# Operands moved by 64 bytes, later spills, batched conditioning and tiles seeded in PSUM in a two-layer diffusion block

## The chip, the cores and the metric

The kernel runs on one core of a Trainium2 chip. The metric is device time in microseconds (us); lower is better. The kernel before took 1252.23, 1252.26 and 1252.82 us in three runs, a median of 1252.26.

Engines are named as in the profile: PE is TensorE's matmul queue and PEld its weight loads, DVE is VectorE, ACT ScalarE, POOL GpSimd, SP SyncE, whose queue issues nearly all of this kernel's DMAs. L123 is line 123 of the kernel.

## The reference, cut to what matters

Two layers work on 512 latent and 256 context tokens of width 1024. Layer 0 mixes tokens by pooling, layer 1 by attention; each is followed by an MLP with 4096 hidden columns. Layer 1 is the last, so its MLP sees latent tokens only.

```python
def ada_mods(cond, w, b):                     # w: 1024 x 6144
    m = (jax.nn.silu(cond) @ w + b)[..., None, :]
    return jnp.split(m, N_MOD, axis=-1)       # sh1, sc1, gt1, sh2, sc2, gt2
...
x = x + gt1 * rms_norm(y_lat, g_mix_post[i])
m_lat = sq_relu_mlp(modulate(rms_norm(x, g_mlp_pre[i]), sh2, sc2), w_mlp_in[i], w_mlp_out[i])
x = x + gt2 * rms_norm(m_lat, g_mlp_post[i])
...
def sq_relu_mlp(h, w_in, w_out):
    return jnp.square(jax.nn.relu(h @ w_in)) @ w_out
```

The conditioning `m` is made for two vectors, `c` (latent) and `c_ctx` (context), and depends on no token. Everything is fp32.

## The kernel before

**Tiles and number format.** Tokens lie in six tiles of 128 (t = 0 to 3 latent, 4 and 5 context). An fp32 product is made of three fp32r matmuls: each operand is split into a rounded `hi` (a ScalarE cast, L120) and a remainder `lo` (a VectorE subtract, L123), and hi·hi, hi·lo and lo·hi are added up in PSUM. A group of 256 hidden columns has w_in and w_out of 1 MB each; there are 16 groups (g).

**Buffers.** `ra` holds the split activations, `rb` the hidden values `hid` and one slot `unit[0]`. A tile `units` holds `unit[1]` and `unit[2]`, two slots of 2 x 2048 columns for split weights. In SBUF `ra`, `rb` and the later tile `sums` begin 32 bytes past a multiple of 128; `units` lies behind a small tile `phase` of 24 floats and begins 96 bytes past one, as do the work tiles, in which the diagonals of `gate_diag` lie too. Raw weights land in `rawp`, three buffers of 1 MB shared by w_in, w_out and w_ada.

**Layer 0's MLP.** The first group and part of the second run as ordinary products (`Inner`, L526). From then on w_in products take seven half-size products in place of eight (`Seven`): `weights_sums(g+1)` builds the combined weights on VectorE (L610 to L620), `sums()` (L561) the combined activations once, and PE multiplies them at L636 with 384 tokens as the moving operand. `out_mm` multiplies the hidden values of a tile with w_out (L731): 12 matmuls with a moving operand of 128x512 into two PSUM banks. `out_ev` adds the banks to `acc` in SBUF on VectorE (L742; a copy, L740, at g = 0). The pool `psB` has four banks, two tiles' worth, which `ada_fin` also uses. w_out of every group is split into `unit[2]`, in one cast and one subtract of 2048 columns. In layer 1 w_out's slots alternate between `ra` (even g) and `units` (odd g).

**Conditioning.** The first 20 pieces of w_ada (256 columns each) run on PE at the start (`ada_mm`, L212; `ada_sel`). The other 28 run on VectorE during layer 0's MLP: `ada_sum` loads 1 MB and makes 7 multiply-adds for each vector (L251), 14 for a dual piece (both vectors), 7 for a lone one (`c` only), then transposes and a reduction (L256). `ada_fin` turns the partial sums into columns with four small fp32 matmuls (L219) and one add (L229). Each g from 0 takes one dual and one lone piece while they last, through `extra0` (ahead of w_in's product) and `mid0` (in its middle); a piece's `ada_fin` comes one step after its sum.

**Spill.** `xr`, the residual stream (six tiles of 512 KB), goes to DRAM during layer 0's MLP, whose `sums` takes its place. The six stores are issued by SP at L703, each at a hand-written time of the list `st`, after the tile's `norm_s`; SP's queue also carries every weight load (L106). L988 loads xr back.

**Order.** The program is written for a scheduler that interleaves the engines' streams by priorities and its own model. Hand-written times (`Steps.at`) fix the order in which steps are handed to it; `keep_in_program_order` pins single instructions. `gate_diag` (L288) turns a gate into two diagonal matrices for matmuls; the one for layer 1's last gate stands in the output stage of attention (L1145).

Of the kernel before, what the change touches and what calls it, by code (L numbers as in the profile page):

```python
# [17 lines left out]
P = 128  # L18
# [35 lines left out]
def backbone(ctx: ExitStack, tc, x, c, ctx_in, c_ctx, w_ada, b_ada, g_mix_pre, g_mix_post,  # L54
# [34 lines left out]
    rb = const.tile([P, 10240], F32R, name="rb")  # L89
    phase = ctx.enter_context(tc.tile_pool(name="phase", bufs=1)).tile([P, 24], F32, name="phase")  # L90
    rawe = ExitStack()
# [22 lines left out]
    def sm_tile(tag):  # L114
        return small.tile([P, 8], F32, tag=tag, name=tag, bufs=2 if tag == "gc" else 8)

    def split(raw, hi, lo, pin=False, pool_hi=False, pool_lo=False, q=None):
        if q is not None:
            raw, hi, lo = (z[:, 512 * q:512 * q + 512] for z in (raw, hi, lo))
        a = gp.tensor_copy(hi, raw) if pool_hi else sc.copy(hi, raw)  # L120
        if pin:
            tc.keep_in_program_order(a)
        b = (gp if pool_lo else ve).tensor_tensor(out=lo, in0=raw, in1=hi, op=ALU.subtract)  # L123
        if pin:
            tc.keep_in_program_order(b)
# [3 lines left out]
    class Ring:  # L129
        def __init__(self, slots):  # L130
            self.slots, self.n = slots, 0

        def load(self, src, width, pin=False, wait=None):
            raw = raw_load(src, width, rawp)
            s = self.slots[self.n % len(self.slots)]
            self.n += 1
            hi, lo = s[:, 0:2048], s[:, 2048:4096]
            if wait is None:
# [64 lines left out]

    rowsd = {}

# [20 lines left out]

    def ada_out(i, m, j, ps, nc_):
        at = m * KT + 2 * j
        ve.tensor_tensor(out=mods[i][:, at:at + 2, 0:nc_], in0=ps.rearrange("p (b c) -> p b c", c=nc_),  # L229
                         in1=cols[:, i * 48 + at: i * 48 + at + 2].unsqueeze(2).broadcast_to([P, 2, nc_]),  # L230
                         op=ALU.add)
        if m in (SC1, SC2):
            s = 0 if m == SC1 else 1
            g0 = 96 + s * 16 + i * KT + 2 * j
            ve.scalar_tensor_tensor(out=avec[i][s][:, 2 * j:2 * j + 2, 0:nc_], in0=mods[i][:, at:at + 2, 0:nc_],
                                    scalar=1.0,
                                    in1=cols[:, g0:g0 + 2].unsqueeze(2).broadcast_to([P, 2, nc_]),
                                    op0=ALU.add, op1=ALU.mult)

    def ada_sum(i, m, j, nc_):  # L240
        raw = raw_load(w_ada[i, :, m * D + j * 256: m * D + (j + 1) * 256]
# [11 lines left out]
        for c, r in enumerate(rows):  # L253
            ve.transpose(raw[:, c, :], r)
        s = small.tile([P, 2, 8], F32, tag="part", name="part", bufs=2)
        ve.tensor_reduce(out=s[:, 0:nc_, :], in_=raw[:, 0:nc_, :].rearrange("p c (g q) -> p c g q", q=32),  # L256
                         axis=AX.X, op=ALU.add)
        rowsd[i, m, j] = s, nc_
# [301 lines left out]

    def sums():  # L561
        held.close()
        S["held"] = ExitStack()
        f = S["held"].enter_context(tc.tile_pool(name="sums", bufs=1, side="right")).tile([P, 8712], F32R, name="sums")[:, 0:8704]
        u = unit[0]
# [131 lines left out]
    for n, t in enumerate(order):  # L697
# [4 lines left out]
        st.at([57.98, 62.18, 66.38, 70.58, 74.78, 78.98][n], norm_s, t, (False, False, False, False, False, False)[n])  # L702
        st.at([61.98, 66.18, 70.38, 74.58, 78.78, 82.98][n], lambda t: sy.dma_start(spill[:, t], xr[:, t]), t)  # L703
        st.at([60.08, 64.28, 68.48, 73.066, 77.266, 81.466][n], norm_c, t, (False, True, False, False, False, False)[n], (False, True, True, True, True, False)[n])
# [8 lines left out]
    def mlp(i, inner, rg, hids, order, extra, mid, last, before_last):  # L713
# [6 lines left out]
        def out_mm(parts, t, cols=HALVES):  # L720
            at_ = place_of[t] if i == 0 else t
            ts_ = slice(at_ * P, (at_ + 1) * P)
            pss = [psB.tile([P, 512], F32, tag="b", name="pso") for _ in cols]
            seq = [(a, f, w) for (_, (hi, lo), (wH, wL)) in parts for f in range(2)
                   for a, w in ((hi, wH), (hi, wL), (lo, wH))]
            order = [(n, h) for n in range(len(seq)) for h in range(len(cols))]
            if len(parts) > 1:
                order.sort(key=lambda z: (z[0] >= (9 if cols == HALVES else 0), z[1]))
            for n, h in order:
                a, f, w = seq[n]  # L730
                te.matmul(pss[h][:, 0:cols[h][1]], a[:, f, ts_], w[:, f, cols[h][0]:sum(cols[h])],  # L731
                          start=(n == 0), stop=(n == len(seq) - 1))
            pso[t] = pss

        def out_ev(parts, t, cols=HALVES):
            pss = pso[t]
            for (c0, w), ps in zip(cols, pss):
                d = accv[:, t, c0:c0 + w]
                if parts[0][0] == 0:
                    ve.tensor_copy(d, ps)  # L740
                else:
                    ve.tensor_tensor(out=d, in0=d, in1=ps[:, 0:w], op=ALU.add)  # L742

        if i == 0:
            one = lambda z: Ring([z])
            wi = w_in(i, 1, one(unit[1]))
# [44 lines left out]
    due = {0: [], 1: []}  # L791

    def ada_step(slot, kinds):
        for u in due[slot]:
            ada_fin(*u[:3])
        due[slot] = [kinds.pop(0)] if kinds else []
        for u in due[slot]:
            ada_sum(*u)

    def mid0(g):  # L800
        ada_step(1, lone)

# [5 lines left out]
    def extra0(g):  # L808
        if g == 1:
            pinned[0] = False  # L810
        if g == 4:
            head_gains()
        ada_step(0, dual or lone)
        if g == NG - 2:
            ada_step(1, [])
        if g == 2:
# [315 lines left out]
    def output(st, base):  # L1132
        at = lambda i, fn, *args: st.at(base + i, fn, *args)
        for n, (ch, t) in enumerate(((0, 0), (0, 1), (1, 0), (0, 2), (1, 1), (0, 3), (1, 2), (1, 3))):
# [3 lines left out]
            if ch:  # L1138
# [19 lines left out]
    def last1(st, n, t):  # L1158
# [3 lines left out]
        st.at(5.2 * n + 7.8, fin_b, t)  # L1162

    mlp(0, first[0], ring, hids0, (4, 5, 0, 1, 2, 3), extra0, mid0, last0, before0)
    mlp(1, first1[0], ring1, hids1, range(NL), lambda g: slot.__setitem__(slice(0, NL), [1] * NL) if g == 3 else None, lambda g: None, last1, lambda: None)


# [50 lines left out]
```

## Time and profile before

| | before |
|---|---|
| runs, us | 1252.23, 1252.26, 1252.82 |
| profiled execution, us | 1250.13 |
| its span in the profile, us | 1248.2 |
| mean granted TensorE clock | 0.985 |
| busy share of the span: PE, DVE, ACT, POOL | 95%, 74%, 42%, 8% |
| instructions | 16629 |

The span runs from the first to the last instruction of the profiled execution; about 2 us of its time lie around it. Times in the trace count from the span's start. The start phase and layer 0's mixer reach to about 120 us, layer 0's MLP to about 690, attention to about 900, layer 1's MLP to the end. A "timeline" row gives start, duration, engine, line, operation, output and inputs, and how many instructions were joined in the row; in brackets stands how long the engine sat idle before and what released it. Durations of joined matmuls overlap the next row by a pipeline's tail, so the spacing of starts is the cost of a matmul. A row of "groups" gives the count, then busy time and mean ns of one, then idle time before them and its releaser. A row of "windows" gives the stretch and its length, then busy time and count of PE, PEld, DVE, ACT and POOL, the granted clock, the share of the DMA engines and GB/s. SPq is SP's queue: its rows are DMA issues, with the waiting of the queue.

### The profile page before, as it was taken

The page shows a single profiled execution, that of the slowest core. Times are in us where ns is not written, and L with a number is a line of the kernel's source. Part 1 is how long each engine was busy: PE and PEld are TensorE (multiplying, and loading weights), DVE is VectorE, ACT ScalarE, POOL GpSimd, SP SyncE. Part 2 cuts the span into 40 slices and gives each one's busy share as a digit, 9 for nine tenths or more (in the row PEclk, how much of TensorE's full clock was granted, in tenths as well). Part 3 has the DMA queues.
Part 4 walks back from the last instruction along what each step waited for, and adds up shares of the span by engine and source line. Part 5 has one row for each costly group of instructions (what it writes and reads, how often), then busy time and mean ns, then how long its engine had stood idle before and what let it go on. Part 6 is the DMA issues. An engine that isn't in the chain of part 4 may idle for free.

```text
span 1248.2 us, 16629 instructions
## 1 busy us (share of the span) xinstructions
PE 1191.6 (95%) x6602; PEld 1017.9 (82%) x6602; DVE 923.5 (74%) x1546; ACT 524.6 (42%) x868; POOL 101.8 (8%) x135
## 2 busy tenths in 40 slices
PE   6889989999999999999999989999999999999997
PEld 5669878888888888888787879988878888888886
DVE  3877998999898999987687589872664554555555
ACT  5666313433333333333476358862632222313222
POOL 1060000000000000000242232001100000000001
PEclk9899989999999999999999989999999999999999
DMA  9985044444444444343521211020233242333201
GB/s 330 345 296 177 1 139 131 135 135 135 136 135 135 135 133 138 124 128 122 198 72 54 82 34 35 1 81 21 68 119 117 70 133 68 103 100 96 73 1 68
DMA packets 105006, 143.71 MB, mean 115 GB/s; under 512 B 2608, under 2 KB 88032, under 8 KB 104928
## 3 DMA queue, kind: packets, MB, share of 16 engines
q1 hardware_dynamic: 104928, 142.64, 35.0%
q8 instruction: 52, 0.85, 0.3%
q14 instruction: 26, 0.21, 0.1%
HBM read 137.39 MB, written 5.24 MB: 114 GB/s over the span
## 4 chain that ended last, share of the span: by engine, by line
PE 78%; DVE 9%; DMA 6%; ACT 3%; issue 1%; POOL 1%; SPq 1%; DVEq 0%; POOLq 0%; ACTq 0%
PE pso L731 30%; PE psin L636 16%; PE psin L526 14%; PE psq L851 5%; DMA raw<-in_w_ada 4%; PE psy L1090 3%; PE po L1064 3%; PE pss L1025 2%; DMA raw<-in_w_mlp_in 2%; PE pspt L1050 1%; ACT junk L146 1%; PE pspool L454 1%; DVE xr L310 1%; PE psada L212 1%; DVE units L123 1%
## 5 line engine op out<-in xcount | busy, mean ns | idle before, releaser
L731 PE MATMUL pso<-units,rb 128*128 128x512 f32 x1542 | 376.6, 396 | 1.9 <-DVE units L123 1.7
L731 PEld LDWEIGHTS pso<-units,rb 128*128 128x128 f32 x1542 | 289.2, 189 | 66.4 <-DVE units L123 2.0
L742 DVE TENSOR_TENSOR acc<-acc,pso 128x512 f32<-128x512 f32 (+1 forms) x281 | 183.7, 680 | 107.2 <-PE pso L731 107.1
L120 ACT CAST units<-raw 128x2048 fp32r<-128x2048 f32 (+1 forms) x46 | 72.7, 1597 | 116.8 <-PE pso L731 95.5
L251 DVE SCALAR_TENSOR_TENSOR rows<-raw,cond,rows 128x256 f32<-128x256 f32 x280 | 117.1, 480 | 0.0
L123 DVE TENSOR_TENSOR units<-raw,units 128x2048 fp32r<-128x2048 f32 (+1 forms) x44 | 86.2, 1972 | 28.1 <-ACT units L120 28.1
L731 PE MATMUL pso<-ra,rb 128*128 128x512 f32 (+1 forms) x390 | 91.1, 386 | 0.0
L157 POOL TENSOR_SCALAR ms<-ss 128x1 f32<-128x1 f32 x21 | 10.5, 502 | 973.2 <-ACT junk L146 972.6
L526 PE MATMUL psin<-ra,units 128*128 128x512 f32 (+1 forms) x320 | 87.5, 375 | 0.0
L731 PEld LDWEIGHTS pso<-ra,rb 128*128 128x128 f32 x390 | 72.6, 188 | 15.2
L526 PE MATMUL psin<-ra 128*128 128x512 f32 x256 | 80.3, 390 | 0.0
L120 ACT CAST ra<-raw 128x2048 fp32r<-128x2048 f32 x16 | 30.4, 1906 | 108.6 <-PE pso L731 82.8
L636 PE MATMUL psin<-ra,units 128*128 128x384 f32 x336 | 66.2, 342 | 1.2 <-ACT psin L648 0.6
L526 PEld LDWEIGHTS psin<-ra,units 128*128 128x128 f32 x320 | 58.7, 188 | 9.3
L636 PE MATMUL psin<-sums,units 128*128 128x384 f32 x336 | 65.4, 342 | 0.5 <-ACT psin L644 0.3
L636 PEld LDWEIGHTS psin<-ra,units 128*128 128x128 f32 x336 | 58.0, 188 | 4.7 <-ACT psin L648 3.2
L636 PEld LDWEIGHTS psin<-sums,units 128*128 128x128 f32 x336 | 57.7, 188 | 3.0 <-ACT psin L644 1.8
L526 PEld LDWEIGHTS psin<-ra 128*128 128x128 f32 x256 | 48.1, 188 | 10.3
L123 DVE TENSOR_TENSOR ra<-raw,ra 128x2048 fp32r<-128x2048 f32 x16 | 36.6, 2291 | 25.2 <-ACT ra L120 25.2
L851 PE MATMUL psq<-units,ra 128*128 128x512 f32 x216 | 53.0, 397 | 0.0
L659 ACT ACTIVATE work<-work 128x768 f32<-128x768 f32 x14 | 11.9, 847 | 91.5 <-DVE work L654 91.5
L526 PE MATMUL psin<-rb,ra 128*128 128x512 f32 x128 | 49.9, 390 | 0.0
(214 smaller groups left out, 2045.5 us busy)
## 6 DMA issues: line engine op xcount, KB each, us to landing
raw<-in_w_ada SPq DMA_DIRECT2D x48, 1024.0 KB, 7.7
raw<-in_w_mlp_in SPq DMA_DIRECT2D x32, 1024.0 KB, 5.5
raw<-in_w_mlp_out SPq DMA_DIRECT2D x32, 1024.0 KB, 5.0
raw<-in_w_qkv SPq DMA_DIRECT2D x6, 1024.0 KB, 5.3
raw<-in_w_o SPq DMA_DIRECT2D x4, 1024.0 KB, 5.1
spill<-xr SPq DMA_DIRECT2D x6, 512.0 KB, 10.5
xr<-spill SPq DMA_DIRECT2D x6, 512.0 KB, 6.9
xr<-in_x SPq DMA_DIRECT2D x4, 512.0 KB, 4.5
```

Of the source, the lines that this page charges most:

```text
L120: a = gp.tensor_copy(hi, raw) if pool_hi else sc.copy(hi, raw)
L123: b = (gp if pool_lo else ve).tensor_tensor(out=lo, in0=raw, in1=hi, op=ALU.subtract)
L146: sc.activation(junk[:, 0:src.shape[-1]], src, AF.Square, scale=float(D) ** -0.5, accum_out=ss)
L251: ve.scalar_tensor_tensor(out=r, in0=raw[:, k, :], scalar=cond[:, k, c:c + 1], in1=r, op0=ALU.mult, op1=ALU.add)
L526: te.matmul(ps[:, bank, o:o + ln], w[:, k, fs], rhs, start=(k == 0 and n == 0), stop=(k == KT - 1 and n == 2))
L636: te.matmul(bank, w[k], a[k], start=start and k == 0 and m == 0, stop=stop and k == 3 and m == 2, skip_group_check=True)
L731: te.matmul(pss[h][:, 0:cols[h][1]], a[:, f, ts_], w[:, f, cols[h][0]:sum(cols[h])], start=(n == 0), stop=(n == len(seq) - 1))
L742: ve.tensor_tensor(out=d, in0=d, in1=ps[:, 0:w], op=ALU.add)
L851: te.matmul(ps, a[:, k, sl], w[:, k % 4, :], start=(k == 0 and n == 0), stop=(k == KT - 1 and n == 2))
L1025: te.matmul(ps[:, c2, 0:384], a[:, sl], b[:, kv, 384 * c2:384 * c2 + 384], start=(n == 0), stop=(n == 2))
L1064: te.matmul(po[:, 0:256], v[:, kt, hs], p[:, kt, qs], start=(kt == 0 and n == 0), stop=(kt == NT - 1 and n == 2))
L1090: te.matmul(ps, a[:, k, sl], w[:, k % 4, o:o + width], start=(k == 0 and n == 0), stop=(k == KT - 1 and n == 2))
```

## The change

1. `phase` grows from 24 to 40 floats, so `units` begins 64 bytes later: 32 bytes past a multiple of 128, as `ra`, `rb` and `sums` do. `sums` gives 192 floats to a new tile `parts`.
2. The rings of layer 0's MLP split a weight in two halves of 1024 columns: cast, subtract, cast, subtract.
3. The six spills leave the list of hand-written times and stand at the head of `sums()`.
4. `ada_sum` writes its partial sums into `parts`, and `ada_fin` runs once for four pieces (one m of one layer) with four times as many columns. Layer 0's MLP takes 24 pieces, from g = 1, a dual and a lone one in turn; the last four (layer 1's GT2) run in layer 1's MLP at g = 4 to 7, their `ada_fin` and `gate_diag` at g = 10.
5. In layer 0, for g > 0, the tiles t = 1 and t = 4 are "seeded" while `stale` is not above zero (an `ada_fin` sets it to 4, every `out_mm` takes 2 off): ScalarE copies acc into the two PSUM banks, the 12 matmuls add to what is there, and ScalarE copies the sum back. The changed kernel has 42 copies each way, so 21 seeded tiles of 84, and 239 adds where there were 281.

```diff
-    phase = ...tile([P, 24], F32, name="phase")
+    phase = ...tile([P, 40], F32, name="phase")
...
+    def split_halves(raw, hi, lo):
+        for q in range(2):
+            z = slice(1024 * q, 1024 * q + 1024)
+            sc.copy(hi[:, z], raw[:, z])
+            ve.tensor_tensor(out=lo[:, z], in0=raw[:, z], in1=hi[:, z], op=ALU.subtract)
...
-    def ada_fin(i, m, j):
-        part, nc_ = rowsd.pop((i, m, j))
+    def ada_fin(i, m, parts, nc_):
+        n = 4 * nc_
         ps = psB.tile([P, 512], F32, tag="b", name="psada")
-        ada_turn(ps[:, 0:2 * nc_], part[:, 0:nc_, :].rearrange("p c (b a) -> p a c b", a=4), nc_)
-        ada_out(i, m, j, ps[:, 0:2 * nc_], nc_)
+        stale[0] = 4
+        for a in range(4):
+            te.matmul(ps[32 * a:32 * a + 32, 0:2 * n], sel,
+                      parts.rearrange("p (u c b a) -> p a u b c", c=nc_, b=2, a=4)[:, a], start=True, stop=True)
+        ada_out(i, m, 0, ps[:, 0:2 * n], nc_, 8)
...
     def sums():
+        for t in (4, 5, 0, 1, 2, 3):
+            sy.dma_start(spill[:, t], xr[:, t])
         held.close()
...
-        st.at([61.98, 66.18, 70.38, 74.58, 78.78, 82.98][n], lambda t: sy.dma_start(spill[:, t], xr[:, t]), t)
...
         def out_mm(parts, t, cols=HALVES):
+            g0 = parts[0][0]
+            seeded[t] = i == 0 and g0 > 0 and len(parts) == 1 and t in (1, 4) and stale[0] <= 0
+            stale[0] -= 2
             pss = [psB.tile([P, 512], F32, tag="b", name="pso") for _ in cols]
+            if seeded[t]:
+                for (c0, w), ps in zip(cols, pss):
+                    sc.copy(ps, accv[:, t, c0:c0 + w])
...
-                          start=(n == 0), stop=(n == len(seq) - 1))
+                          start=(n == 0 and not seeded[t]), stop=(n == len(seq) - 1), skip_group_check=seeded[t])
...
         def out_ev(parts, t, cols=HALVES):
...
+                elif seeded[t]:
+                    sc.copy(d, ps)
...
-            one = lambda z: Ring([z])
+            one = lambda z: Ring([z], True)
...
-    dual = [(0, GT2, j, 2) for j in range(4)] + [(1, m, j, 2) for j in range(4) for m in (SC1, SH1)]
-    lone = [(1, m, j, 1) for m in (GT1, SC2, SH2, GT2) for j in range(4)]
+    dual = [(0, GT2, 2), (1, SC1, 2), (1, SH1, 2)]
+    lone = [(1, m, 1) for m in (GT1, SC2, SH2)]
...
     def mid0(g):
-        ada_step(1, lone)
+        if g:
+            ada_step()
...
-        at(36, gate_diag, 1, GT2, 0, 1)
...
+    def extra1(g):
+        if 3 < g < 8:
+            ada_sum(1, GT2, g - 4, 1, parts[1][:, 8 * g - 32:8 * g - 24])
+        if g == 10:
+            ada_fin(1, GT2, parts[1], 1)
+            gate_diag(1, GT2, 0, 1)
```

Three places in the order of instructions follow; line numbers of the kernel after are its own. **SP's queue at the end of layer 0's mixer**, from the load of the MLP's first w_in on: `raw` is a weight buffer, the `in_` name the weight, `spill` the store of xr. Before:

```order
L106 DMA raw<-in_w_mlp_in 128x8x256
L703 DMA spill<-xr 128x1024
L106 DMA raw<-in_w_ada 128x8x256 x2
L703 DMA spill<-xr 128x1024
L106 DMA raw<-in_w_ada 128x8x256 x2
L703 DMA spill<-xr 128x1024
L106 DMA raw<-in_w_ada 128x8x256
L703 DMA spill<-xr 128x1024 x3
L106 DMA raw<-in_w_mlp_in 128x8x256
L106 DMA raw<-in_w_mlp_out 128x2x1024
```

After:

```order
L106 DMA raw<-in_w_mlp_in 128x8x256
L106 DMA raw<-in_w_ada 128x8x256 x4
L572 DMA spill<-xr 128x1024 x2
L106 DMA raw<-in_w_ada 128x8x256
L572 DMA spill<-xr 128x1024 x3
L106 DMA raw<-in_w_mlp_in 128x8x256
L106 DMA raw<-in_w_mlp_out 128x2x1024
L572 DMA spill<-xr 128x1024
L106 DMA raw<-in_w_mlp_out 128x2x1024
L106 DMA raw<-in_w_mlp_in 128x8x256
```

Four of the five w_ada loads have moved ahead of the first spill, and the loads of g = 1's w_out and g = 2's w_in ahead of any piece of VectorE's conditioning.

**PE where group 0's output meets group 1's hidden values**: `psin` is a w_in product, `pso` an output product, `psada` an `ada_fin`. Before:

```order
L526 MATMUL psin<-ra,units 128x384 x96
L731 MATMUL pso<-units,rb 128x512 x72
L219 MATMUL psada<-part,sel 32x2x2 x4
L219 MATMUL psada<-part,sel 32x2 x4
L731 MATMUL pso<-units,rb 128x512 x18
L636 MATMUL psin<-ra,units 128x384 x2
```

After:

```order
L535 MATMUL psin<-ra,units 128x384 x96
L748 MATMUL pso<-units,rb 128x512 x24
L648 MATMUL psin<-ra,units 128x384 x12
L748 MATMUL pso<-units,rb 128x512 x50
L648 MATMUL psin<-sums,units 128x384 x4
L748 MATMUL pso<-units,rb 128x512 x22
```

The two `ada_fin` that stood behind the 72 matmuls of group 0 are gone, the first of the seven products (12 matmuls) stands among them, and the second (out of `sums`) follows 50 matmuls later.

**ScalarE in the middle of layer 0's MLP**: `units<-raw` is a cast of weights, `ra<-work` of combined weights, `psin` a partial product handed on, `acc` and `pso` the seeds. Before:

```order
L120 CAST units<-raw 128x2048
L618 CAST ra<-work 128x2x4x128
L644 COPY psin<-psin 128x384
L646 COPY work<-psin 128x384
L648 COPY psin<-psin 128x384
L650 ACTIVATE work<-psin 128x384
L659 ACTIVATE work<-work 128x768
L662 ACTIVATE work<-work 128x768
```

After:

```order
L120 CAST units<-raw 128x1024 x2
L630 CAST ra<-work 128x2x4x128
L656 COPY psin<-psin 128x384
L740 COPY pso<-acc 128x512 x2
L658 COPY work<-psin 128x384
L660 COPY psin<-psin 128x384
L759 COPY acc<-pso 128x512 x2
L662 ACTIVATE work<-psin 128x384
L740 COPY pso<-acc 128x512 x2
L671 ACTIVATE work<-work 128x768
```

The copies of the seeds stand between the hand-overs of the seven products, and one pair directly ahead of the activation that waits for VectorE's sum (L659 before, L671 after).

More of the change, by code (lines that the diff above doesn't have):

```diff
@@ L137, in load @@
             hi, lo = s[:, 0:2048], s[:, 2048:4096]
-            if wait is None:
+            if wait is None and self.halves:
+                split_halves(raw, hi, lo)
+            elif wait is None:
                 split(raw, hi, lo, pin)
@@ L202, in backbone @@
     ve.tensor_copy(gpc, pp[:, 128:160])
-    rowsd = {}
+    rowsd, parts, seeded, stale = {}, {}, {}, [0]
     def ada_mm(i, m, j):
@@ L561, in sums @@
     def sums():
+        for t in (4, 5, 0, 1, 2, 3):
+            sy.dma_start(spill[:, t], xr[:, t])
         held.close()
         S["held"] = ExitStack()
-        f = S["held"].enter_context(tc.tile_pool(name="sums", bufs=1, side="right")).tile([P, 8712], F32R, name="sums")[:, 0:8704]
+        pool = S["held"].enter_context(tc.tile_pool(name="sums", bufs=1, side="right"))
+        f, parts[0] = pool.tile([P, 8520], F32R, name="sums"), pool.tile([P, 192], F32, name="parts")
         u = unit[0]
```

54 lines of the change are left out of this document (30 added, 24 removed).

## The prediction

> **What bounds the kernel now.** I read the page first, its busy shares and its 40 slices of 31.2 us:
>
> ```profile
> PE 1191.6 (95%) x6602; PEld 1017.9 (82%) x6602; DVE 923.5 (74%) x1546; ACT 524.6 (42%) x868; POOL 101.8 (8%) x135
> ...
> PE   6889989999999999999999989999999999999997
> ```
>
> PE is busy in 95% of the span. Slices below 9 show where it isn't: the start, above all, the sixth (156 to 187 us), and the end. Then I read four windows, for how hard each engine is loaded in layer 0's MLP (the second and third row) and in layer 1's (the last):
>
> ```profile
> 130.00:180.00 50.00, 42.09 (x205) 36.06 (x204) 48.32 (x93) 13.41 (x16) 0.00 (x0) 0.90 0.26 85
> 300.00:400.00 100.00, 99.19 (x528) 86.44 (x527) 91.12 (x177) 35.80 (x46) 0.00 (x0) 1.00 0.41 127
> 400.00:500.00 100.00, 99.78 (x527) 86.50 (x526) 93.83 (x181) 35.70 (x45) 0.00 (x0) 1.00 0.41 136
> 1000.00:1100.00 100.00, 100.00 (x439) 81.89 (x438) 54.58 (x64) 26.01 (x27) 0.00 (x0) 1.00 0.31 100
> ```
>
> From 300 us on PE is full at full clock, so an edit there is worth exactly what it takes off PE's own instructions, and nothing for what it takes off VectorE: VectorE is at 91 to 94% in layer 0, close to the limit but below PE. In the first row it is the other way round: VectorE has 48.32 of 50 us, PE 42.09. So the change is five sums: two places where PE waits (the start, the hand-over at 130 to 180), two costs on PE itself (how fast a matmul reads its operand, and the small matmuls of `ada_fin`), and one new wait (the seeds).
>
> **The start.** SP's queue and PE, then the norm of the last tiles:
>
> ```profile
> 56.03 3.37 SPq L106 DMA_DIRECT2D raw<-in_w_mlp_in  x1
> 69.69 0.34 SPq L703 DMA_DIRECT2D spill<-xr  x1
> 70.13 1.45 SPq L106 DMA_DIRECT2D raw<-in_w_ada  x2
> ...
> SPq L703 <- DVE xr L310: 15.2, 2, 10.3
> ...
> 87.98 1.07 PE L212 MATMUL psada<-raw,cond 128*32 128x256 f32 x16 [1.76 <-DMA raw<-in_w_ada]
> ...
> 92.13 1.93 PE L212 MATMUL psada<-raw,cond 128*32 128x256 f32 x16 [2.25 <-DMA raw<-in_w_ada]
> ...
> 96.22 0.74 DVE L488 TENSOR_SCALAR acc<-xr,rs 128x1024 f32<-128x1024 f32 x1
> ...
> 110.27 10.10 PE L526 MATMUL psin<-ra,rb 128*128 128x256 f32 x82 [1.57 <-DVE ra L350]
> ...
> 85.00:95.00 10.00, 5.29 (x69) 2.94 (x70) 5.33 (x11) 3.42 (x8) 9.38 (x9) 0.85 1.01 358
> ```
>
> The first spill holds SP's queue from 59.4 (56.03 + 3.37) to 69.69, 10.3 us, until VectorE has made its tile of xr (the row of SP's waits). Two w_ada loads stand right behind it and more behind the next spills; PE waits for them at 87.98 and 92.13. After, four of the five stand ahead of the spills, and 3 MB of spills no longer share the DMA engines (busy share 1.01 in the last row) with them. PE is idle for 10.00 − 5.29 = 4.7 us from 85 to 95, and once more for 1.57 at 110.27: 6.3 that can go. What is late next is the normalised last tile, made at 96.96 (96.22 + 0.74), which no load moves, and POOL, at 9.38 of 10 us. So the bounds are 2 (only the wait of 2.25 goes) and 8 (POOL's work finds room too); I take 6. The spills moved later must land before `sums` is written. Six times 512 KB go out while PE has 24 us of products ahead of it (96.2 to 120.4, where the 82 end), and nothing else asks for xr: nothing.
>
> **The hand-over from group 0 to 1.**
>
> ```profile
> 161.68 0.61 PE L219 MATMUL psada<-part,sel 128*32 128x4 f32 x16 [7.87 <-DVE part L256]
> 162.22 6.67 PE L731 MATMUL pso<-units,rb 128*128 128x512 f32 x18
> 168.72 0.51 PE L636 MATMUL psin<-ra,units 128*128 128x384 f32 x2
> ...
> 159.97 1.09 DVE L254 STREAM_TRANSPOSE raw<-rows 128x256 f32<-128x256 f32 x3
> 160.98 0.97 DVE L256 TENSOR_REDUCE part<-raw 128x16 f32<-128x512 f32 x2
> ...
> 163.69 0.69 DVE L610 TENSOR_TENSOR work<-raw 128x512 f32<-128x512 f32 x1 [1.49 <-DMA raw<-in_w_mlp_in]
> ...
> 167.91 1.22 DVE L603 TENSOR_TENSOR units<-work,units 128x1024 fp32r<-128x1024 f32 x1
> ```
>
> PE waits 7.87 us for VectorE's reduction of a conditioning piece, spends 0.54 on the two `ada_fin`, and then needs 6.50 us for 18 matmuls (162.22 to 168.72) that take 18 x 0.23 = 4.1 at full clock (0.23 is worked out with the operands' place): 2.4 more, in a window whose mean granted clock is 0.90. Together 10.8 us. After, no `ada_fin` stands there; PE has 74 output matmuls and 12 of 384 columns ahead of the first that needs VectorE (second product, combined weights), 74 x 0.23 + 12 x 0.17 = 19.1 us, where it had 72 matmuls, 16.6 us, ahead of its wait. But the combined weights come from VectorE's subtract, which ends at 169.1 here. By the order after, 10 of 21 multiply-adds (0.40 each by a row quoted with the seeds), the three transposes and two reductions no longer stand ahead of it, and w_in, now ahead of the pieces on SP, is loaded in time: 4.0 + 1.09 + 0.97 + 1.49 = 7.6 us less, 161.5. PE ends its 72 at 153.8 (161.68 − 7.87) here, so it gets there at 153.8 − 16.6 + 19.1 = 156.3 and waits 5 to 6, of which I take 6, with the slow clock's 2.4 behind it: 8.4 of 10.8 stay, a gain of 2.4. Bounds: a loss of 2 (VectorE's order worse by a piece's end) and a gain of 8 (its work drawn ahead with the shorter start).
>
> The Trainium skill ("TensorE: Matmul & The Clock Gate", on the clock gate) says that the array falls to half clock after an idle window of about 3.4 us. The rows agree: after 7.87 us of idle the matmuls are slow, after the 1.57 at 110.27 the 82 of half the width take 123 ns each (10.10 / 82), half of 0.23 and a little. By it a wait under 3.4 us would save the 2.4 as well; that lies within the bounds above.
>
> **Operands that begin 64 bytes later.** In layer 1 w_out comes from `ra` for even groups and from `units` for odd ones, with the same stationary values, so that the place of the moving operand alone differs:
>
> ```profile
> 964.76 5.62 PE L731 MATMUL pso<-ra,rb 128*128 128x512 f32 x24
> 970.22 0.62 PE L526 MATMUL psin<-ra,units 128*128 128x512 f32 x2
> ...
> 986.78 5.76 PE L731 MATMUL pso<-units,rb 128*128 128x512 f32 x24
> 992.38 0.62 PE L526 MATMUL psin<-ra 128*128 128x512 f32 x2
> ...
> 870.91 1.09 PE L301 MATMUL psg<-diag,onesr 128*128 128x512 f32 x4
> 871.84 1.91 PE L335 MATMUL psx<-ident,acc 128*128 128x128 f32 x16
> ...
> L731 PE MATMUL pso<-units,rb 128*128 128x512 f32 x1530 | 374.8, 397 | 1.9 <-DVE units L123 1.7
> L851 PE MATMUL psq<-units,ra 128*128 128x512 f32 x216 | 53.0, 397 | 0.0
> L1090 PE MATMUL psy<-units,ra 128*128 128x512 f32 x72 | 17.3, 394 | 0.0
> L1064 PE MATMUL po<-units,rb 128*128 128x256 f32 x288 | 37.3, 283 | 0.5 <-DVE units L1053 0.4
> ```
>
> From start to start, 24 matmuls take 5.46 us from `ra` (227.5 ns each) and 5.60 from `units` (233.3): 5.8 ns more. That is an effect of the place; whether it is the place modulo 128 bytes is my inference. For it speaks that the diagonals lie elsewhere but with the same remainder of 96, and take 0.93 / 4 = 232.5. If so, 1530 + 216 + 72 = 1818 matmuls of 512 columns save 5.8 each, 10.5, and 288 of half the width half of it, 0.8: 11.3, all on a full PE. Bounds 0 (another cause) and 12.7 (0.7 more ns for every such matmul, as stationary reads from `units` may gain too).
>
> The Trainium skill speaks against this term: "TensorE: Matmul & The Clock Gate" (back-to-back gap) gives N ÷ 2.4 GHz + 2.5 ns, 216 ns for 512 columns, without the operand's place. Neither row here is at 216, and two rows with one N differ. "SBUF — State Buffer" (operand start alignment) asks only for a multiple of the element's size and adds that this is about legality and that speed wasn't timed.
>
> **Conditioning in batches.**
>
> ```profile
> L219 PE MATMUL psada<-part,sel x224: 171/192/213, 161.7 to 587.6; 128*32 128x2 f32 x64, 128*32 128x4 f32 x48
> ...
> 554.30 0.86 PE L636 MATMUL psin<-ra,units 128*128 128x384 f32 x4
> 554.99 1.21 PE L636 MATMUL psin<-sums,units 128*128 128x384 f32 x6
> 556.13 0.24 PE L219 MATMUL psada<-part,sel 128*32 128x2 f32 x8
> 556.30 1.31 PE L636 MATMUL psin<-sums,units 128*128 128x384 f32 x6
> ```
>
> The 224 records (weight loads among them) are 28 `ada_fin` of 8. One costs PE 556.30 − 554.99 = 1.31 us less six products at 0.173 (0.69 / 4 in the row ahead), 1.04: 0.27. Two were counted at the hand-over; of the other 26, 7 stay (six in layer 0, one in layer 1), with columns too few to weigh: 19 x 0.27 = 5.1. Four lone pieces (some 4.4 us of VectorE each: eight multiplies at 0.40 to 0.48, a transpose, a reduction) move into layer 1, where VectorE has 45 us of each 100 free; their loads too, at a DMA share of 0.31. `gate_diag`'s 0.93 us moves along. Halved splits cost VectorE and ScalarE a second start, and free the first half earlier: nothing, as long as PE covers them.
>
> **The seeds.**
>
> ```profile
> 72.18 0.58 ACT L302 COPY gate<-psg 128x512 f32<-128x512 f32 x1
> ...
> 372.42 4.84 DVE L251 SCALAR_TENSOR_TENSOR rows<-raw,cond,rows 128x256 f32<-128x256 f32 x12
> ...
> L742 DVE TENSOR_TENSOR acc<-acc,pso 128x512 f32<-128x512 f32 x144 | 95.8, 682 | 16.6 <-PE pso L731 16.5
> ```
>
> Forty-two adds at 0.68 leave VectorE, 28.6 us; 84 copies at some 0.58 come to ScalarE, 49 us, which from 36% goes to about 48%. On a full PE neither is a gain. The wait is new: before, a tile's matmuls needed free banks; now VectorE's add of the tile two back (0.68) and ScalarE's copy (0.58) come first, for two banks some 2.1 us, under the matmuls of the tile between (12 x 0.23 = 2.7). The cover is 0.6; it fails where VectorE is inside a batch of multiply-adds, or ScalarE in another instruction (0.8 or so). I take 2 us over 21 tiles, between 0 and 8.
>
> **The sum.** 6.0 + 2.4 + 11.3 + 5.1 − 2.0 = 22.8. From the profiled execution's 1250.13 (span 1248.2) that is 1227.3. The median of the runs, 1252.26, is 2.1 above the profiled one: 1229.4.
>
> **The rivals.**
>
> *The place is no matter* (chance 0.12): the 5.8 ns come from the region, a bank, say, and not from the remainder modulo 128. Against it stand the diagonals, for it that only one other region shows it. 1229.4 + 11.3 = 1240.7. The skill's formula gives this one.
>
> *The waits stay* (0.11): POOL and the last tile hold the start, VectorE the hand-over, so that only PE's own savings count: 1229.4 + 6 + 2.4 = 1237.8. The window of 130 to 180 speaks for it, the waits for w_ada against it.
>
> *More goes* (0.12): VectorE's relief closes the hand-over's gap and no seed is seen: 8 for 2.4, 0 for 2, 8 for 6 at the start: 1229.4 − 5.6 − 2 − 2 = 1219.8.
>
> *The place and the waits both fail* (0.02): 1249.1, within 0.2% of 1252.3, about what a measurement of this kernel can tell from no change.
>
> *The seeds stall PE* (0.05), the one that ends slower: tile 4's copies wait for VectorE's add, and that stands behind a batch of 4.84. Then PE is late by 4.84 + 2.1 − 2.7 = 4.2; at the 10 or so seeds of tile 4, 42 us, 1229.4 − 2 + 42 = 1269. It decides from (22.8 + 2.0) / 21 = 1.2 us per seeded tile. Against it: VectorE loses 28.6 us of work, and the adds stand between the multiply-adds in its order.
>
> **How the numbers follow.** My forecast has 0.58, with a range of its own of 1222 to 1237. Range: 1219 takes in the far gains, 1241 the place without effect; outside stay the stalling seeds, the double failure and a little beyond the far gains. Faster 0.58 + 0.12 + 0.11 + 0.12 = 0.93, same 0.02, slower 0.05.
>
> **What would show it.** Spacing of `pso<-units` at 227 to 228 ns for 24 matmuls, against 233; seven clusters of psada from `parts` behind the start; the w_ada loads issued from about 59 us and PE at its 82 matmuls some 6 us earlier; a wait for VectorE before the second product of the hand-over; no idle time of PE in front of seeded tiles above 0.2 us. I'm wrong if `units` stays at 233, or if waits on ScalarE's copies add up to more than 8 us.

## The result and the profile after

The changed kernel takes 1220.04 us (median of four runs, 1218.19 to 1220.63); the kernel before took 1252.24 beside it (1251.04 to 1252.82). The ratio is 0.9742, with a 95% interval of 0.9725 to 0.9758: 32.2 us less. The forecast was 22.8 less, at 1229.4, with a range of 1219 to 1241. So the sign and the range held, near the low end, and the sizes did not: what follows is mostly about two of the five terms.

The page of the kernel after, its busy shares and PE's slices (30.5 us each now):

```profile
PE 1172.3 (96%) x6434; PEld 1016.1 (83%) x6434; DVE 903.3 (74%) x1494; ACT 566.6 (46%) x969; POOL 103.5 (8%) x135
...
PE   6799999999999999999989989999899999999997
```

The sixth slice is at 9 tenths now. The windows that were shown of before, of the kernel after (columns as there):

```profile
130.00:180.00 50.00, 48.38 (x223) 41.73 (x222) 39.36 (x64) 18.91 (x28) 0.00 (x0) 0.97 0.19 64
300.00:400.00 100.00, 99.95 (x504) 89.20 (x503) 88.78 (x162) 51.26 (x77) 0.00 (x0) 1.00 0.42 136
400.00:500.00 100.00, 99.00 (x503) 87.68 (x502) 90.17 (x169) 45.34 (x68) 0.00 (x0) 1.00 0.42 137
1000.00:1100.00 100.00, 100.00 (x449) 82.55 (x448) 58.20 (x76) 27.28 (x27) 0.00 (x0) 1.00 0.29 99
85.00:95.00 10.00, 8.29 (x81) 7.04 (x78) 9.22 (x16) 9.69 (x23) 9.48 (x7) 1.00 0.88 300
```

In the first row VectorE has 39.36 of 50 us where it had 48.32, and PE 48.38 where it had 42.09. In the next two ScalarE carries 45 to 51 where it had 36, and VectorE 89 to 90 where it had 91 to 94. In the last row, at the end of the mixer, PE is idle for 1.7 us where it was for 4.7, at a clock of 1.00 where it had 0.85.

Where the time went is read by setting the same point of PE's program side by side. Before, on PE (the 96 products of 384 columns ahead of the hand-over, and the seventh of the first seven products behind it):

```profile
120.21 16.80 PE L526 MATMUL psin<-ra,units 128*128 128x384 f32 x96
...
194.08 2.36 PE L636 MATMUL psin<-ra 128*128 128x384 f32 x12
```

After:

```profile
112.56 16.91 PE L535 MATMUL psin<-ra,units 128*128 128x384 f32 x96
...
178.49 2.27 PE L648 MATMUL psin<-ra 128*128 128x384 f32 x12
```

The start is 7.65 us shorter (120.21 − 112.56). From there to the seventh product, with the same 144 output matmuls in both, it is 73.87 before and 65.93 after, 7.9 less. That leaves 13.9 of the 29.5 by which the span fell (1248.2 to 1218.7), in the rest of layer 0 and in layer 1.

### The profile page after: what moved, and what is told of

It is laid out like the page before. It is cut to its first block, busy times and chain, and to the rows that moved or that the text cites. A ratio compares the mean times of both kernels' runs of the same rounds, so it can differ in the third digit from the quotient of the medians.

```text
span 1218.7 us, 16348 instructions
## 1 busy us (share of the span) xinstructions
PE 1172.3 (96%) x6434; PEld 1016.1 (83%) x6434; DVE 903.3 (74%) x1494; ACT 566.6 (46%) x969; POOL 103.5 (8%) x135
## 4 chain that ended last, share of the span: by engine, by line
PE 41%; DVE 3%; issue 3%; ACT 2%; POOL 2%; POOLq 0%; DVEq 0%; ACTq 0%
PE pso L748 14%; PE psin L535 14%; PE psy L1115 3%; PE po L1089 3%; PE pss L1050 2%; PE psq L876 2%; PE pspt L1075 1%; ACT junk L154 1%; DVE xr L319 1%; POOL rs L885 1%; DVE work L901 0%; POOL ms L165 0%; POOL rs L167 0%; PE psx L344 0%; DVE units L1078 0%
## 5 line engine op out<-in xcount | busy, mean ns | idle before, releaser
L748 PE MATMUL pso<-units,rb 128*128 128x512 f32 x1542 | 369.8, 391 | 2.3 <-DVE units L129 1.2
L761 DVE TENSOR_TENSOR acc<-acc,pso 128x512 f32<-128x512 f32 x239 | 155.4, 681 | 91.4 <-PE pso L748 91.0
L259 DVE SCALAR_TENSOR_TENSOR rows<-raw,cond,rows 128x256 f32<-128x256 f32 x280 | 124.5, 483 | 1.0
L126 ACT CAST units<-raw 128x2048 fp32r<-128x2048 f32 (+1 forms) x29 | 40.3, 1417 | 93.6 <-PE pso L748 76.5
L129 DVE TENSOR_TENSOR units<-raw,units 128x2048 fp32r<-128x2048 f32 (+1 forms) x27 | 47.8, 1796 | 18.8 <-ACT units L126 18.8
L740 ACT COPY pso<-acc 128x512 f32<-128x512 f32 x42 | 24.3, 589 | 65.2 <-DVE acc L761 65.2
```

The source lines that it names most:

```text
L259: ve.scalar_tensor_tensor(out=r, in0=raw[:, k, :], scalar=cond[:, k, c:c + 1], in1=r, op0=ALU.mult, op1=ALU.add)
L740: sc.copy(ps, accv[:, t, c0:c0 + w])
```

## The experiments

**The place of the operands.** Four kernels keep every engine's order of instructions and change only where `units` begins. The first is the kernel before with the change's first part alone:

```diff
-    phase = ...tile([P, 24], F32, name="phase")
+    phase = ...tile([P, 40], F32, name="phase")
```

> The kernel before with phase at 40 floats and nothing else, so that units begins 32 bytes past a multiple of 128 and every engine's order of instructions stays. Theory A (the remainder modulo 128 sets how fast a 512-column moving operand is read): 24 matmuls from units take 5.46 us and the time falls by 11.3 us, to about 1241. Rival B (the region or something else sets it): 5.60 us stay and the time is that of before, 1252.

It took 1244.7 us, ratio 0.994 (0.992 to 0.996): 7.3 less than before. The second takes the part away from the kernel after:

```diff
-    phase = ...tile([P, 40], F32, name="phase")
+    phase = ...tile([P, 24], F32, name="phase")
```

> The kernel after with phase back at 24 floats, order the same. Theory A: about 11 us slower than after, 1231. Rival B: as after, 1220. If the term is larger than forecast and so explains the extra gain of 7 to 9 us (rival C): 1238 or more.

1228.23 us, ratio to before 0.9807 (0.9777 to 0.9838): 8.2 more than after. So the place counts, by 7 to 8 us; the two ways of asking agree. The forecast's 11.3 lies outside the first interval (5 to 10 us) and not outside the second, whose four runs scatter from 1223 to 1231. Two more put `units` on a multiple of 128 and 64 bytes past one:

```diff
-    phase = ...tile([P, 40], F32, name="phase")
+    phase = ...tile([P, 32], F32, name="phase")
```

> The kernel after with phase at 32 floats: units begins on a multiple of 128, ra and rb 32 bytes past one. Theory A in the form 'same remainder as the stationary operand' gives something slower than after, by up to 11 us (1220 to 1231); in the form 'the remainder 96 alone is slow' 1220. Rival B: 1220.

```diff
-    phase = ...tile([P, 40], F32, name="phase")
+    phase = ...tile([P, 48], F32, name="phase")
...
-    ... pool.tile([P, 8520], F32R, name="sums")
+    ... pool.tile([P, 8488], F32R, name="sums")
```

> The kernel after with phase at 48 floats (and sums 32 floats shorter at its unused end, to make room): units begins 64 bytes past a multiple of 128. Theory A, same remainder: 1220 to 1231; 'the remainder 96 alone' (or 'less than 64 bytes of the first 128'): 1220 for 96 alone. Rival B: 1220.

1230.09 us (0.9818, 0.9793 to 0.9843) and 1228.19 us (0.9811, 0.9792 to 0.9829): both as slow as the remainder of 96. So 96 is not a bad place by itself; either 32 is a good one, or what is good is that it is `rb`'s, which holds the stationary operand. The fifth kernel tells these apart, by moving all three:

```diff
-    ra = const.tile([P, 2 * KT * TOK], F32R, name="ra")
+    pad = const.tile([P, 8], F32, name="pad"); ra = const.tile([P, 2 * KT * TOK], F32R, name="ra")
...
-    ... pool.tile([P, 8520], F32R, name="sums")
+    ... pool.tile([P, 8488], F32R, name="sums")
```

> The kernel after with ra, rb and units all moved to 64 bytes past a multiple of 128 (a pad of 8 floats ahead of ra; sums at 32 as before), order the same. Theory A1 (what counts is that moving and stationary operand have the same remainder): 227 ns per matmul of 512 columns and the time of after, 1220. Rival A2 (32 is the fast place for a moving operand): 233 ns and 1228, as with 0, 64 and 96.

1219.36 us, ratio 0.9743 (0.973 to 0.9756): as fast as after. It is the relation between the two operands. PE's timeline shows it at the matmul, 24 output matmuls from `units` and the row behind them, in the kernel after (units, rb at 32):

```profile
948.88 5.60 PE L748 MATMUL pso<-units,rb 128*128 128x512 f32 x24
954.32 0.39 PE L535 MATMUL psin<-ra 128*128 128x512 f32 x1
```

with units at 0 and rb at 32:

```profile
953.98 5.76 PE L748 MATMUL pso<-units,rb 128*128 128x512 f32 x24
959.58 0.39 PE L535 MATMUL psin<-ra 128*128 128x512 f32 x1
```

and with all at 64:

```profile
947.72 5.60 PE L748 MATMUL pso<-units,rb 128*128 128x512 f32 x24
953.16 0.39 PE L535 MATMUL psin<-ra 128*128 128x512 f32 x1
```

From start to start 5.44, 5.60 and 5.44 us, 226.7, 233.3 and 226.7 ns each. Before itself, where 96 and 32 agree modulo 64 and are slow, excludes a modulus of 64: of four places of `units`, 32 bytes apart, only one is fast. So 128 is the smallest modulus that fits, and not shown to be the one; larger ones were not tried. Neither value is the 216 ns without regard to place that the Trainium skill ("TensorE: Matmul & The Clock Gate", back-to-back gap) gives; here the measurement decides.

Why 7 to 8 and not 11 is read from the groups by shape of the first kernel of this set; the rows of before stand with the prediction (374.8, 53.0, 17.3 and 37.3 us):

```profile
L731 PE MATMUL pso<-units,rb 128*128 128x512 f32 x1530 | 367.2, 392 | 1.8 <-DVE units L123 1.7
L851 PE MATMUL psq<-units,ra 128*128 128x512 f32 x216 | 51.9, 392 | 0.0
L1090 PE MATMUL psy<-units,ra 128*128 128x512 f32 x72 | 16.8, 389 | 0.0
L1064 PE MATMUL po<-units,rb 128*128 128x256 f32 x288 | 38.2, 287 | 0.5 <-DVE units L1053 0.4
```

The 1818 matmuls of 512 columns lost 7.6, 1.1 and 0.5 us, 9.2 where the forecast had 10.5: some 5 ns each, less than the 6.6 of the undisturbed 24 (why is not shown). And matmuls of half the width went the other way. The 288 of the last row took 0.9 us more, and the 48 of layer 1's attention output 0.3, first in before and then in this kernel:

```profile
L1090 PE MATMUL psy<-units,ra 128*128 128x256 f32 x48 | 5.7, 278 | 0.0
```

```profile
L1090 PE MATMUL psy<-units,ra 128*128 128x256 f32 x48 | 6.0, 284 | 0.0
```

That is 1.2 us more where the forecast had 0.8 less. Together it makes 9.2 − 1.2 = 8.0, which the runs' 7.3 and 8.2 fit.

**The spills.** Put back between the w_ada loads:

```diff
     def sums():
-        for t in (4, 5, 0, 1, 2, 3):
-            sy.dma_start(spill[:, t], xr[:, t])
...
+        st.at([61.98, 66.18, 70.38, 74.58, 78.78, 82.98][n], lambda t: sy.dma_start(spill[:, t], xr[:, t]), t)
```

> The kernel after with the spills back at their hand-written times, between the w_ada loads. Theory S (the first spill holds SP's queue for 10 us, and PE waits for the loads behind it): the start is 6 to 7.6 us longer, 1226 to 1228. Rival (the start's gain comes from elsewhere, POOL and the last tile set its end): 1220 to 1221.

1227.13 us, ratio 0.9806 (0.979 to 0.9821): 7.1 more than after. SP's queue in the kernel after:

```profile
54.80 3.38 SPq L106 DMA_DIRECT2D raw<-in_w_mlp_in  x1
58.27 12.53 SPq L106 DMA_DIRECT2D raw<-in_w_ada  x4
70.85 3.45 SPq L572 DMA_DIRECT2D spill<-xr  x2
```

and with the spills put back, where the queue is silent from 58.77 to 69.94 again; below it the same point of PE's program as above:

```profile
55.39 3.38 SPq L106 DMA_DIRECT2D raw<-in_w_mlp_in  x1
69.94 0.34 SPq L713 DMA_DIRECT2D spill<-xr  x1
70.38 1.45 SPq L106 DMA_DIRECT2D raw<-in_w_ada  x2
...
121.12 16.81 PE L535 MATMUL psin<-ra,units 128*128 128x384 f32 x96
```

PE arrives there at 121.12 against 112.56: all of the start's gain is the place of the spills in SP's queue.

**Conditioning from group 0.**

```diff
     def mid0(g):
-        if g:
-            ada_step()
+        ada_step()
...
-        if g:
-            ada_step()
+        ada_step()
```

> The kernel after with the conditioning on VectorE from g = 0, as before, batches and all else as after. Theory H (the two pieces of g = 0 stand ahead of the combined weights on VectorE, and hold the raw buffer of w_in): the wait at the hand-over comes back, over 3.4 us, with slow matmuls behind it, 1226 to 1229. Rival (the wait was the two ada_fin's alone, which batching took away; or the order of PE): at most 2 us of wait, 1220 to 1222.

1227.36 us, ratio 0.9809 (0.9795 to 0.9822): 7.3 more than after, as the theory's number had it, but not in the way it said. PE's timeline, its waits at the hand-over and at the same seventh product (the last row):

```profile
147.59 11.65 PE L748 MATMUL pso<-units,rb 128*128 128x512 f32 x46 [0.70 <-ACT pso L740]
...
172.41 2.38 PE L648 MATMUL psin<-ra,units 128*128 128x384 f32 x12 [1.38 <-ACT psin L660]
...
181.17 2.36 PE L648 MATMUL psin<-ra 128*128 128x384 f32 x12 [2.22 <-DVE work L664]
```

No wait is over 3.4 us, and the seventh product comes at 181.17 against 178.49: 2.7 us of the 7.3 are lost at the hand-over. Another 4.2 are lost between there and attention's first product (621.67 against 614.74 after). PE's window from 180 to 560 us has 376.47 of 380 busy:

```profile
180.00:560.00 380.00, 376.47 (x1898) 335.86 (x1899) 322.34 (x592) 177.22 (x264) 0.00 (x0) 1.00 0.38 125
```

After, it is 378.95 (below). Of the 3.5 idle here 1.2 are the wait of the last row above, so 1.3 more than after's 1.05 come later; and for 3.4 us, from 409.2, the clock is at half (0.57 over 409 to 413), which costs 1.7. The remaining 1.2, and what in the pieces' earlier place brings these waits, the runs don't tell. And even so the stretch is 5.1 us shorter than in the kernel before (181.17 − 112.43 = 68.74 against 73.87): with the pieces back, but in batches, no `ada_fin` stands in PE's queue at the hand-over, behind which outputs would wait for VectorE's reduction. That this makes the 5.1 (less 0.7 for the operands' place) is read from the order and wasn't tried by itself.

**The seeds.** None at all:

```diff
-            seeded[t] = ... and t in (1, 4) and stale[0] <= 0
+            seeded[t] = ... and t in () and stale[0] <= 0
```

> The kernel after with no tile seeded: all 281 adds on VectorE. Theory N (the seeds take nothing off PE and cost little): 1218 to 1220. Rival R (the batches alone leave VectorE too full, and the seeds' 28.6 us of relief are what keeps PE from waiting): 1223 or more, with PE's idle time in layer 0 up by 3 us or more.

1229.48 us, ratio 0.9823 (0.9809 to 0.9836): 9.4 more than after, where the forecast had the seeds cost 0 to 8. VectorE's load alone, taken down by other means, in a kernel that leaves out a part of the conditioning's sums:

```diff
-            seeded[t] = ... and t in (1, 4) and stale[0] <= 0
+            seeded[t] = ... and t in () and stale[0] <= 0
...
-        for k in range(1, KT):
+        for k in range(1, KT - 2):
```

> No tile seeded, and two of the seven multiply-adds of each conditioning vector left out (so a part of the conditioning's sum over the input is missing): some 72 instructions of 0.4 us, 29 us, leave VectorE in layer 0's MLP, as much as the 42 adds that the seeds take away, and nothing comes to ScalarE. Theory V (the seeds gain because they relieve VectorE): 1219 to 1222. Rival P (they gain by what they do to PSUM banks or to the order, not by VectorE's load): 1227 to 1230, as with no seeds.

1216.63 us, ratio 0.9713 (0.9699 to 0.9726). The same window of the four kernels that tell this, from 180 to 560 us, in the order before, after, no seeds, no seeds with smaller sums (busy time of PE, PEld, DVE, ACT, POOL, then the clock):

```profile
180.00:560.00 380.00, 378.82 (x2026) 331.70 (x2025) 349.37 (x659) 141.14 (x179) 0.00 (x0) 1.00 0.41 131
```

```profile
180.00:560.00 380.00, 378.95 (x1917) 339.04 (x1916) 333.15 (x617) 182.47 (x273) 0.00 (x0) 1.00 0.40 132
```

```profile
180.00:560.00 380.00, 373.49 (x1869) 330.47 (x1868) 346.78 (x644) 138.27 (x188) 0.00 (x0) 1.00 0.40 131
```

```profile
180.00:560.00 380.00, 380.00 (x1937) 341.74 (x1936) 331.52 (x590) 146.99 (x198) 0.00 (x0) 1.00 0.41 133
```

With 346.78 on VectorE PE has 6.5 us of idle time; with 333.15 it has 1.05, with 331.52 none. The copies on ScalarE have no part in the last, so it is VectorE's load that counts. Shorter sums also let go of their raw buffer sooner, which this run doesn't separate. Of the 9.4 us some 5.5 are idle time in this window, and 1.7 a stretch of 3.4 us at half clock behind some of the waits (0.57 over 375 to 379); the rest was not traced. And the groups of the kernel without seeds say what PE waits for:

```profile
L748 PE MATMUL pso<-units,rb 128*128 128x512 f32 x833 | 204.0, 395 | 2.4 <-DVE units L121 1.3 <-ACT units L120 0.7 <-DVE acc L761 0.2
L648 PE MATMUL psin<-ra,units 128*128 128x384 f32 x288 | 56.2, 340 | 2.5 <-DVE units L615 1.4 <-ACT units L614 1.1
...
L648 PE MATMUL psin<-ra 128*128 128x384 f32 x132 | 25.1, 338 | 0.8 <-DVE work L664 0.8
```

They are splits of weights, VectorE's subtracts (L121, L615) and the ScalarE casts ahead of them (L120, L614), and hardly any add into acc. That they are late because VectorE is full is my reading. Before had as much on VectorE (349.37) and PE nearly always busy. I read it so, without a run of its own: there PE spent more on its own instructions in a group, with the small matmuls and the slower operands, and VectorE had that much longer for the same work. Then as many seeds as the rule on stale banks lets through:

```diff
-            seeded[t] = ... and t in (1, 4) and stale[0] <= 0
+            seeded[t] = ... and stale[0] <= 0
```

> The kernel after with every tile seeded that the rule on stale banks allows: 136 copies each way (68 tiles) in place of 42. VectorE loses another 64 us, ScalarE gains 109 us. Theory V with room left: PE has some 3 us of idle time in layer 0's MLP, so 1217 to 1220. Rival R2 (each seeded tile makes PE wait for the chain add or copy, copy, matmul, 1.2 us and more a tile where two seeded tiles follow each other): 1270 or more.

1219.7 us, ratio 0.9736 (0.9723 to 0.9749): no different from after. The window, and the copies' row:

```profile
180.00:560.00 380.00, 379.16 (x1927) 340.72 (x1926) 289.75 (x533) 265.22 (x445) 0.00 (x0) 1.00 0.41 133
```

```profile
L740 ACT COPY pso<-acc 128x512 f32<-128x512 f32 x122 | 71.7, 606 | 18.1 <-DVE acc L761 18.0
```

ScalarE waits 18.0 us for VectorE's adds, and PE for almost nothing: the rival by which seeds stall PE falls even with 68 of them. Forty-two copies each way are enough; more relief by seeds gains nothing. Both stay some 3 us above the 1216.63 without seeds and with smaller sums, so the seeds may cost something, as the forecast had it, beside their larger gain; no run separates the two.

**Batches.** One `ada_fin` for each piece, without seeds (which a fresh `ada_fin` in every group would not allow):

```diff
-            if j == 3:
-                due.append((2, i, m, parts[0][:, at:at + 32 * nc_], nc_))
+            due.append((1, i, m, j, parts[0][:, at + 8 * nc_ * j:at + 8 * nc_ * j + 8 * nc_], nc_))
```

> No tile seeded, and one ada_fin for each piece (24 in layer 0 in place of 6), all else as after. To be held against the kernel without seeds, 1229.5. Forecast's price: 18 more at 0.27, 4.9 us, 1234. Rival (where VectorE sets the pace, PE's small matmuls fall into waits and cost nothing): 1229 to 1231.

1233.06 us, ratio 0.9845 (0.9832 to 0.9859): 3.6 more than without seeds by the medians, between the forecast's price and the rival's, with intervals that just overlap. Part of it is not `ada_fin`'s own time: PE's idle time from 180 to 560 us is 8.2 against 6.5, and the clock is at half twice (from 279.9 and from 413.0) where it was once. One group has most of the waits, for VectorE's part of the combined weights:

```profile
L655 PE MATMUL psin<-ra,units 128*128 128x384 f32 x288 | 59.5, 351 | 6.4 <-DVE units L622 5.8 <-ACT psin L667 0.6
...
L278 PE MATMUL psada<-parts,sel 128*32 128x2 f32 (+1 forms) x184 | 4.9, 180 | 0.4 <-DVE acc L768 0.4
```

**Whole splits.**

```diff
-            one = lambda z: Ring([z], True)
+            one = lambda z: Ring([z])
```

> The kernel after with w_out split whole (one cast, one subtract of 2048 columns). Forecast's term: nothing, 1219 to 1221. Rival (PE waits for the first half of w_out, as it does for a cast of units at the hand-over, 0.46 us): some tenths per group, 1222 to 1226.

1222.99 us (1220.3 to 1224.97), ratio 0.9762 (0.9748 to 0.9776): 3 more by the medians, but the intervals of this ratio and of after's overlap. The trace has the wait that the rival names, at the hand-over:

```profile
149.80 0.73 PE L748 MATMUL pso<-units,rb 128*128 128x512 f32 x2 [1.99 <-ACT units L126]
...
152.91 3.26 PE L748 MATMUL pso<-units,rb 128*128 128x512 f32 x13 [0.66 <-DVE units L129]
```

1.99 us where after has 0.46 (below). By these runs the halves are worth up to 3 us, and that they are worth nothing is not excluded.

## Why the prediction was right, and where its sizes were wrong

**The start**, 6.0 forecast, 7.65 in the profile and 7.1 by the runs. The mechanism held, and POOL and the last tile did not stop it: the gain is near the bound of 8 that I gave to "POOL's work finds room too". The sum counted only idle time; the same window had PE at a clock of 0.85 before and has it at 1.00 after.

**The hand-over**, 2.4 forecast. Of the 7.9 measured, 1.0 belongs to other terms (144 matmuls at 5 ns, and a later `ada_fin` of 0.27 in the stretch): some 7. The step that failed is "waits 5 to 6, of which I take 6". PE after, and below it VectorE's subtract:

```profile
148.43 0.73 PE L748 MATMUL pso<-units,rb 128*128 128x512 f32 x2 [0.46 <-ACT units L120]
150.33 1.60 PE L648 MATMUL psin<-sums,units 128*128 128x384 f32 x4 [1.16 <-ACT units L614]
151.72 6.15 PE L748 MATMUL pso<-units,rb 128*128 128x512 f32 x22
157.71 3.65 PE L648 MATMUL psin<-sums,units 128*128 128x384 f32 x20
```

```profile
153.38 1.25 DVE L615 TENSOR_TENSOR units<-work,units 128x1024 fp32r<-128x1024 f32 x1
```

My two arrival times were good. With the start's 7.65 taken off, PE should come at 148.7 and VectorE's subtract be done at 153.9; PE is through its 74 outputs at about 149, and the subtract ends at 154.6. But PE did not need the subtract there. The four matmuls of the second product that stand in the order ahead of 22 outputs run on the rounded part, which ScalarE's cast (L614) has made at 150.3, and are done before the subtract begins at 153.38; the subtract is needed by the 20 behind, at 157.71, and the 22 outputs cover it. That was in the order of the changed kernel, shown ahead of the prediction: 4, then 22. The wait is 1.62 us instead of 6, and 1.7 at a slow clock follow where I had 2.4 (more on that at the end).

**The operands' place**, 11.3 forecast, 7.3 and 8.2 by the runs. The mechanism was right in that the place counts, and narrower than I put it: it is the two operands' relation. The size was off: some 9.2 for the wide matmuls where I had 10.5, and 1.2 lost with the half-width ones where I had 0.8 gained.

**Batches**, 5.1 forecast; 3.6 for 18 of the 19 in the one comparison, with waits mixed in and intervals that overlap. That agrees in size and is not resolved further.

**The seeds**, a cost of 2.0 forecast, a gain of 9.4 measured. The step that failed is "on a full PE neither is a gain". I compared VectorE's load of before with PE's load of before, 91 to 94% against 99%, and let the other three edits shorten PE's side without asking what they made of VectorE's share. The kernel without seeds came out at 1229.48, close to the 1227.4 that the other terms gave, but by offsetting errors: more from the start and the hand-over, less from the operands, and PE waiting for VectorE by several microseconds that I had not counted. "More goes" of the rivals came nearest in its time, 1219.8; its reason, that no seed is seen, is not the one found. That 1220.04 lies inside the range, by 1.0 us, is in part luck: the lower end was drawn for far gains at the start and the hand-over, and the largest single gain stood in the sum as a cost.

The experiments undo one part each, and their sum (7.1 + 7.3 + 8.2 + 9.4, and what batches and halves give) is larger than 32.2, so they can't be added. I take it that a full VectorE pays for several of them at once; no run undoes two of these parts together to show it, save the batches and the seeds.

## What to carry to other kernels

When several edits take time off the engine that is full, work out the load of the second one anew against the shortened first: here an engine at 91 to 94% became the one that the full engine waits for as soon as that had given up some 2% (1252 to 1229 us), and work moved off it then counted. Before a wait is priced, look in the order for which operand the next instruction needs, the rounded half or the remainder, and for what stands between. In a queue shared by loads and stores, a store that waits for its data holds every load behind it: here 10 us of SP's queue were 7 us of the kernel.

## What the runs showed of the hardware that was not expected

A matmul with a 512-column moving operand takes 226.7 ns where its moving and its stationary operand have the same remainder modulo 128 bytes in SBUF (32 and 32, 64 and 64; larger moduli are not excluded), and 233.3 where the moving one is at 96, 0 or 64 and the stationary one at 32. With 256 columns the sign was the other way: mean durations of 278 and 283 ns with `units` at 96, 284 and 287 at 32, for the 48 and the 288 above.

The stationary operand can be the one in `units` too, which the forecast had only in a bound: it is so in 336 matmuls of layer 1's w_in products, whose moving operand lies at 32. The larger group of them, with `units` at 96 (before), at 32 (after) and at 0:

```profile
L526 PE MATMUL psin<-ra,units 128*128 128x512 f32 x224 | 70.7, 392 | 0.0
```

```profile
L535 PE MATMUL psin<-ra,units 128*128 128x512 f32 x224 | 70.6, 389 | 0.0
```

```profile
L535 PE MATMUL psin<-ra,units 128*128 128x512 f32 x224 | 71.9, 395 | 0.0
```

At 0 the mean duration is 6 ns longer than at 32, as with the roles the other way; at 96 it is only 3 longer. So the relation counts in both roles, but "same remainder or not" is not the whole rule.

The clock fell after less idle time than the forecast's rule had it. A row of the forecast showed this already: from 85 to 95 us before's clock is 0.85, and no wait there is over 2.25 us. In each of the fourteen profiles all changes of the granted clock lie on one grid of 3.41 us, and where the grid begins differs from one execution to the next. In the kernel after, the grid's step from 147.00 to 150.41 holds both waits of the hand-over, 1.62 us of idle time, and the next step is at half clock:

```profile
147.00:150.41 3.41, 1.79 (x8) 0.86 (x6) 3.41 (x8) 3.08 (x4) 0.00 (x0) 1.00 0.00 0
150.41:153.82 3.41, 3.41 (x9) 2.98 (x10) 3.41 (x6) 1.85 (x3) 0.00 (x0) 0.50 0.65 198
```

With all operands at 64 the same two waits, 0.46 and 1.16 us, are parted by the grid, and the clock stays:

```profile
146.30:149.71 3.41, 2.79 (x12) 1.66 (x10) 3.41 (x8) 1.99 (x3) 0.00 (x0) 1.00 0.00 0
149.71:153.13 3.42, 2.42 (x11) 1.95 (x12) 3.42 (x5) 2.94 (x5) 0.00 (x0) 1.00 0.26 80
```

Four more profiles have this pair of waits: with `units` at 0 and with the spills put back one step holds it whole (1.60 us idle), and half clock follows; with `units` at 96 and at 64 it is parted, and the clock stays. So it was the luck of the grid in the profiled execution that took 1.7 us of the kernel after (the four products and 22 outputs behind took 7.38 us, 150.33 to 157.71, where 4 x 0.174 + 22 x 0.228 = 5.7 would do at full clock). No sharp border in idle time comes out of these traces: one step of 1.88 us of idle time (859.70 to 863.11, all operands at 64) was followed by full clock.

The Trainium skill ("TensorE: Matmul & The Clock Gate", on the clock gate) puts the drop after an idle window of about 3.4 us. The length agrees with the grid's step of 3.41; that PE must be idle through the whole of it does not hold here, where 1.60 us were enough.
